# Low-rank and gate weights of an RWKV-7 mixer split in two once, kept in DRAM, and multiplied in one-pass products

## Chip, core and metric

The kernel runs on one core of one Trainium2 chip. The metric is the device time of one execution in microseconds (us). TensorE (PE in the profile) does the matrix products, VectorE (DVE), ScalarE (ACT) and GpSimd (POOL) the elementwise work; SyncE (SP) and ACT issue transfers (DMA).

## What is computed

One layer of a hybrid decoder for 256 prompt tokens and 8 tokens of sequences that go on, 264 columns in all: a SwiGLU feed-forward (2048 to 5504 to 2048), a mixing stage in which sliding-window attention and an RWKV-7 recurrence stand side by side, and a second feed-forward. The part that the change is about, cut from the reference:

```python
wl, al, gl = xm[..., o3:o4], xm[..., o4:o5], xm[..., o5:]          # 64, 64 and 128 columns
w = -softplus(-(w0 + tanh(wl) @ w2)) - 0.5                         # w2: 64 x 1024, decay
logw = -exp(w)
a = sigmoid(a0 + al @ a2)                                          # a2: 64 x 1024, rate
g = sigmoid(gl) @ g2                                               # g2: 128 x 1024, gate
...
out = (yn + bonus) * g
```

All numbers are float32, so each weight matrix is used at nearly float32 precision.

## The kernel before

Activations lie transposed: 128 features in the partitions, 264 tokens along a row. A weight block of 128 x 128 is the stationary side of a product, the 264 tokens the moving side.

**Large products** (`gemm`, with `chunk`) split both sides. `chunk` loads up to 512 columns of weights (256 KB) on SP's queue into a ring `raw` of 6, rounds them on ACT into `hi` (type fp32r, which TensorE takes in one pass), and subtracts `hi` on DVE to get `lo`; `hi` and `lo` are rings of 4 tiles each. The activations are split in the same way, once, by the norms. Each 128 x 128 block then takes three one-pass products (line 84 in the profile, as all products): hi by hi, hi by the activations' low part, lo by hi. A full chunk feeds 12 products. As the rings have 4 tiles, a chunk's rounding can start as soon as PE has finished with the fourth chunk before it.

**The first feed-forward** runs in six parts (`PARTS`) of 7 or 8 blocks of the inner width. For each block f it multiplies 2 x 16 weight blocks (gate and up), then for the part the down projection. From the second part on, each f also copies one row block of the key and value caches from DRAM to DRAM on ACT's queue (`copy_one`, line 230), 16 copies in all.

**The mixing stage** (`mixing_body`) projects the normed input tile by tile (`win`, `shifted`), in the order of the list `SEQ`. The first two tiles are the low-rank and gate inputs: `la` (64 rows for decay, 64 for rate) and `sgl`. `tw` gets tanh of the first 64 rows of `la`, and a 65th row of ones that adds w0; `sgl` gets the sigmoid. The 16 heads are worked in 8 pairs, two pairs to a batch. For each pair a task `prep` loads its weights with `load` (a ring `ld` of `NLD` = 6 tiles, from SP's queue) and makes two plain float32 products, `zp` (decay, 65 rows) and `ap` (rate, 128 rows of which 64 are zero in the weights). Each batch's `chain` then solves a triangular system with many small DVE steps (tiles X, Xt, st, TT, PT), and its `gnorm` at the end makes one float32 gate product `gp` per pair. All small products write to a ring `m` of 5 PSUM banks, the large ones to a ring `acc` of 3.

**Order.** Tasks are generators; `tick` after each chunk of a large product advances each by one step, and constants such as `PW`, `PZ` and `LAG` say how many ticks a task waits. From this text a scheduler of the tile framework, with its own timing of engines, orders each engine's instructions. `high_priority` puts a weight chunk's steps ahead of others. Each engine then runs its list in order, waiting on semaphores.

The lines of the float32 products and of the loads:

```python
lw = load(I["lw"][p], (P, 256))
mm(zp[:, :T], lw[0:65, 0:P], tw[0:65, :])
mm(ap[:, :T], lw[:, P:2 * P], la)
...
mm(gp[:, :T], g2s[k], sgl)
```

Of the kernel before, what the change touches and what calls it, by code (L numbers as in the profile page):

```python
# [28 lines left out]
NACC, NM = 3, 5  # L29
NH, NQ, NT, NLD = 16, 8, 16, 6  # L30
ROW = 320
# [19 lines left out]
VG1, VGM, VG2, VGF = 0, 16, 32, 48  # L51
VMU, VKK, VKA, VA0, VRK, VLW, VLB, VSK, VSD = 64, 90, 98, 106, 114, 122, 130, 138, 154
NVEC = 155
CID, CBO, CCM, CMK = 0, 128, 256, 384


def body(tc, I, O):
# [51 lines left out]
    with ExitStack() as ctx:  # L109
# [21 lines left out]
        def mp():  # L131
            return pp.tile([P, 512], F32, tag="m", bufs=NM, name=uid("m"))
# [95 lines left out]
        def copy_one():  # L228
            n, c, b = copies.pop()
            tc.keep_in_program_order(A.dma_start(O[n][b, 0:127, :], I[c][b, 1:128, :]))  # L230

        def hblock(nf):
            h = cur[0][0].tile([P, max(PARTS), 2, ROW], F32R, tag="h", bufs=2, name=uid("h"))
            return [(h[:, k, 1, :T], h[:, k, 0, :T]) for k in reversed(range(nf))]

        def ffn(nrm, xr, gu, dn, nxt, load, begin=None, side=None, ready=None, end=None):
            rstd = None
            f0 = 0
            for pi, nf in enumerate(PARTS):
# [25 lines left out]
                for f in range(f0 + n0 if first else f0, f0 + nf):  # L265
# [9 lines left out]
                    if begin and pi and copies:  # L275
                        copy_one()
                    if side and pi:
                        next(side, None)
# [90 lines left out]
        def mixing_body(mx, n2, n3, XD, XR):  # L369
            def fix(shape, name):  # L370
                return mx.tile(list(shape), F32, name=name)
# [15 lines left out]
            wc = fix((P, NPAIR, 4), "wc")  # L387
            tw = fix((65, T), "tw")
            G.memset(tw[64:65, :], 1.0)
            rs = fix((P, T), "rs")  # L390
# [5 lines left out]
            for i in range(4):  # L396
                G.tensor_copy(unit[i * 32:i * 32 + 32, :], ident[i * 32:i * 32 + 32, i * 32:i * 32 + 32])
            half = fix((P, 16), "half")
            ts(V, half, vec[:, VKA:VKA + 16], 0.5, ALU.mult)
            less = fix((P, 8), "less")  # L400
# [28 lines left out]

            la, sgl = fix((P, T), "la"), fix((P, T), "sgl")  # L430

# [6 lines left out]
            def prep(p, bt, k, xrr, xk, xv):  # L438
                lw = load(I["lw"][p], (P, 256))
                zp = mp()  # L440
                mm(zp[:, :T], lw[0:65, 0:P], tw[0:65, :])
                ap = mp()
                mm(ap[:, :T], lw[:, P:2 * P], la)
                sg, a = tmp(), tmp()
                act(sg, zp[:, :T], AF.Tanh, scale=0.5)
                ts(G, sg, sg, 0.5, ALU.mult, 0.5, ALU.add)
# [116 lines left out]
            def chain(bt):  # L563
# [119 lines left out]
                for k in range(n):  # L683
                    A.dma_start(O["wkvp"][bt.p0 + k], S[:, k])
                g2s = [load(I["g2"][bt.p0 + k], (P, P)) for k in range(n)]
                yield from gnorm(bt, pY, N, g2s)
# [15 lines left out]
            def gnorm(bt, pY, N, g2s):  # L702
# [26 lines left out]
                for k in range(n):  # L729
                    p, o = bt.p0 + k, yb[bt.p0 + k]  # L730
                    gp = mp()
                    mm(gp[:, :T], g2s[k], sgl)
                    o4, b4 = (x[:, :NP].rearrange("p (q e t) -> p q e t", q=2, e=2) for x in (o, bt.bv[k]))
                    t4 = tp[:, k * NP:(k + 1) * NP].rearrange("p (q g t) -> p q g t", q=2, g=2)
                    for e in range(2):
                        for h in range(2):
                            r = HALF[h]
                            stt(o4[r, :, e, :], t4[HALF[e], :, 1 - h, :], vc(VLW + p)[r], b4[r, :, e, :], ALU.mult, ALU.add)
                    stt(o[:, NP:], sq[:, k * NB:(k + 1) * NB], vc(VLW + p), bt.bv[k][:, NP:], ALU.mult, ALU.add)
                    stt(o, o, vc(VLB + p), gp[:, :T], ALU.add, ALU.mult)  # L740
                    mixed[p] = o
# [162 lines left out]

            shifted(0, la)
            act(tw[0:64, :], la[0:64, :], AF.Tanh)
            shifted(1, sgl)
            act(sgl, sgl, AF.Tanh, scale=0.5)
            ts(G, sgl, sgl, 0.5, ALU.mult, 0.5, ALU.add)
            bat, att, bts, scores = [], [], [], []  # L910
            for kind, i in SEQ:
# [84 lines left out]
        def second_ffn(n3, xr, XR):  # L996
# [6 lines left out]
            with tc.tile_pool(name="f2", bufs=1) as fp:  # L1003
# [70 lines left out]
                for e, q, o, n, r in ((V, SP, 0, 1, rp[:, :T]), (V, A, 1, 3, rp[:, :T]), (G, SP, 4, 4, rb), (V, A, 12, 4, rp[:, :T])):  # L1074
# [3 lines left out]
                    q.dma_start(O["yT"][:, d:d + n, :], y)  # L1078

        xsp = [dp.tile([P, T], F32, tag=f"xsp{o}", name=f"xsp{o}") for o in range(KD)]  # L1080
        xs4 = [blk(f"x{i}", 8, F32R) for i in (3, 2, 1, 0)]
# [36 lines left out]
def layout(i):  # L1118
# [3 lines left out]
    for n in (1, 2):  # L1122
# [12 lines left out]
        v(i["ffn1_norm"][0]), v(i["mix_norm"][0]), v(i["ffn2_norm"][0]), v(i["final_norm"]),  # L1135
        v(i["shift_mu"][0][sc]), v(i["key_k"][0]), v(i["key_a"][0]), v(i["aaa_a0"][0]),
        v(i["bonus_r_k"][0].reshape(-1)), v(i["ln_x_w"][0]), v(i["ln_x_b"][0]),
# [6 lines left out]
    a["shs"] = c(i["state_shift"][0][:, sc].reshape(NB, NSH, P).transpose(2, 1, 0))  # L1144
    lw = np.zeros((8, P, 256), f4)
    lw[:, :64, :P] = i["decay_w2"][0].reshape(64, 8, P).transpose(1, 0, 2)
    lw[:, 64, :P] = i["decay_w0"][0].reshape(8, P)
    lw[:, 64:, P:] = i["aaa_a2"][0].reshape(64, 8, P).transpose(1, 0, 2)
    a["lw"] = lw
    a["g2"] = c(i["gate_g2"][0].reshape(P, 8, P).transpose(1, 0, 2))  # L1150
    bk = _buckets()
# [39 lines left out]
```

## Time and profile before

| | |
|---|---|
| median of 3 runs | 1935.38 us (1935.24 to 1937.05) |
| profiled execution, its own time | 1934.77 us |
| its span, first to last instruction | 1932.9 us |
| granted TensorE clock | 0.998 of full |
| first feed-forward | to about 757 us |
| mixing stage with its output projection | about 757 to 1236 us |
| second feed-forward and final norm | from about 1236 us |
| moved by DMA | 357 MB, 185 GB/s |

A row of a timeline reads: start in us, duration in us, engine, line of the kernel, operation, output tile <- input tiles (buffer numbers left out), shapes, and how many instructions were merged. In brackets stands how long the engine sat idle before, and what released it. Matmul rows overlap, since a product is shown until its last column has left the array: what one costs is read from start to start. A float32 product is recorded as two rows. "PEld" is the loading of the stationary side. "SPq" and "ACTq" rows are the issue of a transfer, not the transfer.

### The profile page before, as it was taken

Reading aid. Unit: us, or ns where it says so; the run is one execution under the profiler, and the core shown is the slowest. Engines: PE = TensorE matmul, PEld = TensorE weight load, DVE = VectorE, ACT = ScalarE, POOL = GpSimd, SP = SyncE. Lnnn points to the kernel's source line nnn. Section 1 sums busy time; section 2 is a strip of 40 time slices with the busy share of each in tenths; the row PEclk is TensorE's granted clock in tenths of the full one; section 3 lists DMA queues with packets and bytes.
Section 4 is the critical chain, followed back from the end, with each engine's and each line's share of the span. In section 5 each row is a group of like instructions: output and inputs, shape, how many; then the busy total and the mean of one; then the engine's idle time right before and its main releaser. Section 6 shows DMA issues by size and latency. Waiting matters only on the chain.

```text
span 1932.9 us, 45519 instructions
## 1 busy us (share of the span) xinstructions
PE 1919.4 (99%) x17171; PEld 1897.1 (98%) x17171; DVE 1311.8 (68%) x2606; ACT 1023.7 (53%) x2034; POOL 260.1 (13%) x376
## 2 busy tenths in 40 slices
PE   9999999999999999999999999999999999999998
PEld 9999999999999999999989999999999999999998
DVE  5865555655556568889988977866666666666665
ACT  5644444444444457675657555644444444444446
POOL 0401101011010113222102100300101001010012
PEclk9999999999999999999999999999999999999999
DMA  7666666666666668555646656666666666666664
GB/s 241 178 192 196 185 195 195 183 192 177 190 183 180 188 181 238 177 165 153 176 120 165 210 155 183 175 188 188 189 195 195 186 192 189 194 195 184 193 181 150
DMA packets 218464, 357.27 MB, mean 185 GB/s; under 512 B 33516, under 2 KB 71804, under 8 KB 218244
## 3 DMA queue, kind: packets, MB, share of 16 engines
q1 hardware_dynamic: 211936, 346.02, 60.8%
q10 hardware_dynamic: 6308, 8.35, 1.4%
q8 instruction: 134, 2.20, 0.4%
q14 instruction: 86, 0.70, 0.1%
HBM read 346.67 MB, written 9.69 MB: 184 GB/s over the span
## 4 chain that ended last, share of the span: by engine, by line
PE 96%; DVE 1%; ACT 1%; issue 1%; DMA 0%; POOLq 0%; POOL 0%; ACTq 0%; DVEq 0%
PE acc L84 89%; PE m L84 6%; DVE lo L68 0%; ACT t L78 0%; ACT hi L141 0%; DMA x<-in_x 0%; DVE t L801 0%; DVE st L68 0%; DVE Xt L68 0%; DMA ld<-in_bias 0%; ACT BT L533 0%; ACT L78 0%; POOLq L1187 0%; DVE PT L68 0%; PE m L528 0%
## 5 line engine op out<-in xcount | busy, mean ns | idle before, releaser
L68 DVE TENSOR_TENSOR lo<-raw,hi 128x512 fp32r<-128x512 f32 (+1 forms) x1288 | 874.0, 682 | 510.4 <-ACT hi L141 486.9
L141 ACT CAST hi<-raw 128x512 fp32r<-128x512 f32 (+1 forms) x1288 | 776.8, 606 | 820.2 <-PE acc L84 745.2
L84 PE MATMUL acc<-x,hi 128*128 128x264 f32 x4840 | 893.4, 286 | 0.8 <-ACT hi L141 0.8
L84 PEld LDWEIGHTS acc<-x,hi 128*128 128x128 f32 x4840 | 750.1, 189 | 4.3 <-ACT hi L141 1.0
L84 PE MATMUL acc<-x,lo 128*128 128x264 f32 x2420 | 691.3, 286 | 0.2 <-DVE lo L68 0.2
L84 PE MATMUL acc<-h,hi 128*128 128x264 f32 x2752 | 495.0, 284 | 0.0
L84 PEld LDWEIGHTS acc<-x,lo 128*128 128x128 f32 x2420 | 457.2, 189 | 2.7 <-issue 0.7
L84 PEld LDWEIGHTS acc<-h,hi 128*128 128x128 f32 x2752 | 424.4, 189 | 0.0
L84 PE MATMUL acc<-h,lo 128*128 128x264 f32 x1376 | 387.8, 284 | 0.0
L84 PEld LDWEIGHTS acc<-h,lo 128*128 128x128 f32 x1376 | 259.2, 189 | 0.0
L68 POOL TENSOR_TENSOR t<-t,t 128x264 f32<-128x264 f32 x74 | 79.8, 1078 | 1096.1 <-DVE t L68 949.8
L84 PE MATMUL acc<-y,hi 128*128 128x264 f32 x648 | 122.7, 284 | 0.0
L84 PE MATMUL acc<-o,hi 128*128 128x264 f32 x648 | 120.1, 284 | 0.0
L84 PE MATMUL acc<-kv,hi 128*128 128x264 f32 x582 | 109.8, 285 | 0.0
L84 PEld LDWEIGHTS acc<-y,hi 128*128 128x128 f32 x648 | 101.2, 189 | 0.1
L84 PEld LDWEIGHTS acc<-o,hi 128*128 128x128 f32 x648 | 100.1, 189 | 0.0
L71 DVE SCALAR_TENSOR_TENSOR x<-acc,x 128x264 f32<-128x264 f32 (+1 forms) x193 | 81.1, 425 | 24.3 <-PE acc L84 23.4
L84 PE MATMUL acc<-y,lo 128*128 128x264 f32 x324 | 92.0, 284 | 0.0
L84 PE MATMUL acc<-o,lo 128*128 128x264 f32 x324 | 92.0, 284 | 0.0
L84 PEld LDWEIGHTS acc<-kv,hi 128*128 128x128 f32 x582 | 89.9, 189 | 0.2
L68 DVE TENSOR_TENSOR t<-acc,t 128x264 f32<-128x264 f32 x156 | 67.4, 432 | 32.9 <-PE acc L84 32.9
L84 PE MATMUL acc<-kv,lo 128*128 128x264 f32 x291 | 82.9, 285 | 0.0
(307 smaller groups left out, 1592.5 us busy)
## 6 DMA issues: line engine op xcount, KB each, us to landing
raw<-in_gu SPq DMA_DIRECT2D x688, 256.0 KB, 3.4
raw<-in_dn SPq DMA_DIRECT2D x224, 256.0 KB, 2.9
raw<-in_win SPq DMA_DIRECT2D x152, 256.0 KB, 3.4
raw<-in_dn SPq DMA_DIRECT2D x160, 192.0 KB, 2.8
raw<-in_wout SPq DMA_DIRECT2D x64, 256.0 KB, 3.5
xsp<-x ACTq DMA_DIRECT2D x16, 132.0 KB, 3.4
x<-xsp SPq DMA_DIRECT2D x16, 132.0 KB, 4.2
ld<-in_sT SPq DMA_DIRECT2D x16, 128.0 KB, 3.6
```

Of the source, the lines that this page charges most:

```text
L68: return e.tensor_tensor(out=out, in0=a, in1=b, op=op)
L71: return V.scalar_tensor_tensor(out=out, in0=a, scalar=s, in1=b, op0=op0, op1=op1)
L84: return TE.matmul(out, lhsT, rhs, start=start, stop=stop, **k)
L141: A.copy(hi[:, :w], raw[:, :w])
```

## The change

Three things. The weights of the three small products are put in one tensor `low` of 128 x 3072: eight pairs of 256 columns, the decay and rate weights of each pair, each of the two stacked twice over the 128 rows (64 rows and the same 64 again), then 1024 columns of the gate. While the first feed-forward is in its fourth part, six calls of `low_one` take it through `chunk` in pieces of 512 columns and store both parts in a DRAM tile `low`. In mixing, the inputs are split too: `lor[0]` holds the high part of tanh(wl) in rows 0 to 63 and its low part in rows 64 to 127, `lor[1]` the same for `al`; `gate[0]` and `gate[1]` are the high and low part of the gate's input. A pair's decay and rate products are then two one-pass products each (the high and the low weights by the stacked input), the gate's are three. w0 comes in as a bias of the tanh on ACT, halved in advance. `NLD` is 8 instead of 6, and each load fetches one part (128 KB).

```diff
-NH, NQ, NT, NLD = 16, 8, 16, 6
+NH, NQ, NT, NLD = 16, 8, 16, 8
...
+        lows = list(range(6))
+
+        def low_one():
+            q = lows.pop(0)
+            for e, x in enumerate(chunk(I["low"][:, q * 512:(q + 1) * 512], CH, V)):
+                A.dma_start(low[:, 2 * q:2 * q + 2, e], x.bitcast(F32).rearrange("p (k c) -> p k c", k=2))
...
                     if begin and pi and copies:
                         copy_one()
+                    if begin and pi > 2 and lows:
+                        low_one()
...
-            tw = fix((65, T), "tw")
-            G.memset(tw[64:65, :], 1.0)
...
-            half = fix((P, 16), "half")
-            ts(V, half, vec[:, VKA:VKA + 16], 0.5, ALU.mult)
+            half = vec[:, VKA:VKA + 24]
+            ts(V, half, half, 0.5, ALU.mult)
...
-            la, sgl = fix((P, T), "la"), fix((P, T), "sgl")
+            lor = blk("e", 2, F32R)
+            gate = [mx.tile([P, T], F32R, name=f"gate{i}") for i in range(2)]
+
+            def parts(src):
+                return [load(src[:, e], (P, 256)).bitcast(F32R) for e in range(2)]
...
-                lw = load(I["lw"][p], (P, 256))
-                zp = mp()
-                mm(zp[:, :T], lw[0:65, 0:P], tw[0:65, :])
-                ap = mp()
-                mm(ap[:, :T], lw[:, P:2 * P], la)
+                lw = parts(low[:, p])
+                zp, ap = mp(), mp()
+                for j, ps in enumerate((zp, ap)):
+                    for i, w in enumerate(lw):
+                        mm(ps[:, :T], w[:, j * P:(j + 1) * P], lor[j], i == 0, i == 1)
                 sg, a = tmp(), tmp()
-                act(sg, zp[:, :T], AF.Tanh, scale=0.5)
+                act(sg, zp[:, :T], AF.Tanh, scale=0.5, bias=half[:, 16 + p:17 + p])
...
-                g2s = [load(I["g2"][bt.p0 + k], (P, P)) for k in range(n)]
+                g2s = parts(low[:, NPAIR + bt.i])
...
-                    mm(gp[:, :T], g2s[k], sgl)
+                    c = slice(k * P, (k + 1) * P)
+                    mm(gp[:, :T], g2s[0][:, c], gate[0], True, False)
+                    mm(gp[:, :T], g2s[0][:, c], gate[1], False, False)
+                    mm(gp[:, :T], g2s[1][:, c], gate[0], False, True)
...
-            shifted(0, la)
-            act(tw[0:64, :], la[0:64, :], AF.Tanh)
-            shifted(1, sgl)
+            la = shifted(0, tmp())
+            act(la[0:64, :], la[0:64, :], AF.Tanh)
+            for r, x in zip(HALF, lor):
+                A.copy(x[0:64], la[r])
+                tt(V, x[64:128], la[r], x[0:64].bitcast(F32), ALU.subtract)
+            sgl = shifted(1, tmp())
             act(sgl, sgl, AF.Tanh, scale=0.5)
             ts(G, sgl, sgl, 0.5, ALU.mult, 0.5, ALU.add)
+            A.copy(gate[0], sgl)
+            tt(V, gate[1], sgl, gate[0].bitcast(F32), ALU.subtract)
...
+        low = dp.tile([P, NPAIR + len(BATCH), 2, 256], F32, tag="low", name="low")
```

The scheduler makes a new order of it. Three places follow; `hi_`, `raw_` and the like with a number are single buffers of the rings. First ACT's list where the fourth part of the first feed-forward begins, before and then now:

```order
L141 CAST hi_5337<-raw_5336 128x512
L141 CAST hi_5355<-raw_5354 128x384
L230 DMA out_ks<-in_ck 16x2032
L141 CAST hi_5375<-raw_5374 128x512
L141 CAST hi_5393<-raw_5392 128x512
```

```order
L141 CAST hi_5338<-raw_5337 128x512
L141 CAST hi_5356<-raw_5355 128x384
L230 DMA out_ks<-in_ck 16x2032
L141 CAST hi_5376<-raw_5375 128x512
L237 DMA low<-hi_5376 128x2x256
L141 CAST hi_5384<-raw_5383 128x512
L237 DMA low<-lo_5377 128x2x256
L141 CAST hi_5402<-raw_5401 128x512
```

The first chunk after the cache copy is now one of the split weights; its high part is stored at once, its low part behind the next chunk's cast. The five further splits stand in the same way, one in each of the following five blocks f.

Second, ACT's list at the start of the mixing stage, before and then now. The tile `la` is `t_10482` in the changed kernel, `e` is the tile of `lor`:

```order
L78 ACTIVATE la<-pj_10406,vec 128x256
L141 CAST hi_10638<-raw_10637 128x512
L78 ACT_TABLE_LOAD
L78 ACTIVATE tw<-la 64x264
L141 CAST hi_10656<-raw_10655 128x512
L78 ACTIVATE sgl<-pj_10407,vec 128x256
L141 CAST hi_10681<-raw_10680 128x512
L78 ACTIVATE sgl<-sgl 128x264
L141 CAST hi_10699<-raw_10698 128x512
```

```order
L78 ACTIVATE t_10482<-pj_10453,vec 128x256
L433 COPY t_10570<-ss 128x8
L141 CAST hi_10693<-raw_10692 128x512
L78 ACT_TABLE_LOAD
L78 ACTIVATE t_10482<-t_10482 64x264
L922 CAST e_10475<-t_10482 64x264 x2
L141 CAST hi_10711<-raw_10710 128x512
L78 ACTIVATE t_10570<-pj_10454,vec 128x256
L433 COPY t_10654<-ss 128x8
L141 CAST hi_10736<-raw_10735 128x512
L78 ACTIVATE t_10570<-t_10570 128x264
L141 CAST hi_10754<-raw_10753 128x512
```

Two casts of 64 x 264 now stand between the tanh and the weight cast behind it. On DVE the two subtractions of 64 x 264 stand ahead of that chunk's subtraction.

Third, PE's list in the first batch, from the last of its Gram products (`kr` by `bk`) to the transposes of `kr` and `bk` (lines 521 and 528 before, 532 and 539 now); rows of `acc` are large products. Before and then now:

```order
L84 MATMUL m_11379<-kr_11262,bk_11261 128x128
L84 MATMUL acc_11345<-x_108,hi_11427 128x264
L84 MATMUL acc_11345<-x_108,lo_11428 128x264
L84 MATMUL acc_11345<-x_108,hi_11427 128x264 x2
L84 MATMUL acc_11345<-x_108,lo_11428 128x264
L84 MATMUL acc_11345<-x_108,hi_11427 128x264 x2
L84 MATMUL acc_11345<-x_108,lo_11428 128x264
L84 MATMUL acc_11345<-x_108,hi_11427 128x264 x2
L84 MATMUL acc_11345<-x_108,lo_11428 128x264
L521 MATMUL m_11444<-C,kr_10968 128x128 x2
L528 MATMUL m_11451<-C,bk_10967 128x128 x4
```

```order
L84 MATMUL m_11442<-kr_11325,bk_11324 128x128
L532 MATMUL m_11507<-C,kr_11027 128x128 x2
L84 MATMUL acc_11408<-x_110,lo_11541 128x264
L84 MATMUL acc_11408<-x_110,hi_11540 128x264 x2
L84 MATMUL acc_11408<-x_110,lo_11541 128x264
L84 MATMUL acc_11408<-x_110,hi_11540 128x264 x2
L84 MATMUL acc_11408<-x_110,lo_11541 128x264
L539 MATMUL m_11514<-C,bk_11026 128x128 x4
```

The Gram products stand 13 large products later than before, and the first transposes follow them at once instead of after 11 large products. The small products of the other batches move by up to about 16 large products.

More of the change, by code (lines that the diff above doesn't have):

```diff
@@ L51 @@
 VG1, VGM, VG2, VGF = 0, 16, 32, 48
-VMU, VKK, VKA, VA0, VRK, VLW, VLB, VSK, VSD = 64, 90, 98, 106, 114, 122, 130, 138, 154
-NVEC = 155
+VMU, VKK, VKA, VA0, VW0, VRK, VLW, VLB, VSK, VSD = 64, 90, 98, 106, 114, 122, 130, 138, 146, 162
+NVEC = 163
 CID, CBO, CCM, CMK = 0, 128, 256, 384
@@ L1135, in layout @@
         v(i["ffn1_norm"][0]), v(i["mix_norm"][0]), v(i["ffn2_norm"][0]), v(i["final_norm"]),
-        v(i["shift_mu"][0][sc]), v(i["key_k"][0]), v(i["key_a"][0]), v(i["aaa_a0"][0]),
+        v(i["shift_mu"][0][sc]), v(i["key_k"][0]), v(i["key_a"][0]), v(i["aaa_a0"][0]), v(i["decay_w0"][0].reshape(-1)),
         v(i["bonus_r_k"][0].reshape(-1)), v(i["ln_x_w"][0]), v(i["ln_x_b"][0]),
@@ L1144, in layout @@
     a["shs"] = c(i["state_shift"][0][:, sc].reshape(NB, NSH, P).transpose(2, 1, 0))
[L1145 to L1150, printed above, removed]
+    w2, a2 = (i[n][0].reshape(64, 8, P) for n in ("decay_w2", "aaa_a2"))
+    low = np.stack([np.concatenate([x, x], 0) for x in (w2, a2)], 2).reshape(P, 2 * 8 * P)
+    a["low"] = c(np.concatenate([low, i["gate_g2"][0]], 1))
     bk = _buckets()
```

## Prediction

> **What bounds the kernel now.** I read the page's busy times first, then its chain of work, then a table of busy times by stage, then the waits of TensorE (PE).
>
> ```profile
> PE 1919.4 (99%) x17171; PEld 1897.1 (98%) x17171; DVE 1311.8 (68%) x2606; ACT 1023.7 (53%) x2034; POOL 260.1 (13%) x376
> PE 96%; DVE 1%; ACT 1%; issue 1%; DMA 0%; POOLq 0%; POOL 0%; ACTq 0%; DVEq 0%
> 66.00:757.00 691.00, 691.00 (x5760) 691.00 (x5759) 418.99 (x711) 344.28 (x619) 89.45 (x89) 1.00 0.64 190
> 757.00:870.00 113.00, 112.85 (x1042) 110.16 (x1042) 92.20 (x191) 76.93 (x186) 30.62 (x79) 1.00 0.61 179
> 870.00:990.00 120.00, 117.72 (x1558) 110.19 (x1555) 110.80 (x371) 75.27 (x203) 20.51 (x52) 1.00 0.55 156
> 990.00:1100.00 110.00, 109.40 (x1240) 100.77 (x1239) 94.15 (x278) 73.72 (x202) 19.07 (x45) 1.00 0.61 173
> 1100.00:1180.00 80.00, 80.00 (x879) 78.39 (x878) 62.86 (x136) 38.74 (x70) 1.02 (x1) 1.00 0.59 165
> PE m L808 <- DVE PT L68: 1.2, 1, 1.2
> PE m L755 <- issue: 0.7, 1, 0.7
> PE m L84 <- ACT kr L544: 0.2, 1, 0.2
> ```
>
> In the table by stage the columns are stretch, length, then busy us (and instructions) of PE, PEld, DVE, ACT and POOL, then PEclk, DMA share and GB/s. PE is the bound: 99% of the span is busy and 96% of the chain is its own work, at the full clock. The first feed-forward (up to 757) has no idle PE at all. The mixing stage (757 to 1180), where the low-rank and gate products are, has about 3 us of it, in single waits such as the three shown. So a shorter product on PE shortens the program, as long as no other engine is late for what comes next. DVE is the nearest: 110.8 of 120 us busy between 870 and 990.
>
> **Removed and added products.** Eight channel pairs have two FP32 products each (decay and rate) and one for the gate: 24 in all. These rows show four of them in a row, two of the gate and the two of pair 6 (a product leaves two records).
>
> ```profile
> 1028.35 1.06 PE L84 MATMUL m<-sgl,ld 128*128 128x264 f32 x4
> 1029.24 0.61 PE L84 MATMUL m<-tw,ld 65*128 65x264 f32 x2
> 1029.69 0.61 PE L84 MATMUL m<-la,ld 128*128 128x264 f32 x2
> 1029.94 0.48 PE L84 MATMUL acc<-x,lo 128*128 128x264 f32 x1
> 1030.25 0.40 PE L84 MATMUL acc<-x,hi 128*128 128x264 f32 x2
> ```
>
> From start to start, two gate products take 1029.24 - 1028.35 = 0.89 us, the decay product 1029.69 - 1029.24 = 0.45: 0.445 each. A one-pass product takes 691.00 / 5760 = 0.120 us, its weight load hidden beside the one before; this is also the form of every added product (128 rows, 264 columns). Removed: 24 x 0.445 = 10.7 us. Added: decay and rate 2 each per pair, since high and low halves of the activations lie stacked over 128 rows, and 3 for the gate: 8 x (2 + 2 + 3) = 56, times 0.120 = 6.7 us. On PE that is **-4.0 us**: -0.41 per pair for decay and rate, -0.085 for the gate.
>
> The rows say that FP32 costs 3.7 times one pass. [...]
>
> **The weights' split in the first feed-forward.** Six more chunks go through the rings raw, hi and lo: 6 loads on SP's queue, 6 casts on ACT, 6 subtractions on DVE, 12 stores on ACT's queue. PE multiplies nothing with them. Each takes one of four hi/lo slots, so PE's weights are ready one chunk later than now.
>
> ```profile
> 389.74 0.62 ACT L141 CAST hi<-raw 128x512 fp32r<-128x512 f32 x1 [0.82 <-PE acc L84]
> 390.39 0.69 DVE L68 TENSOR_TENSOR lo<-raw,hi 128x512 fp32r<-128x512 f32 x1 [0.75 <-ACT hi L141]
> 391.18 0.62 ACT L141 CAST hi<-raw 128x512 fp32r<-128x512 f32 x1 [0.82 <-PE acc L84]
> 401.82 0.52 ACTq L230 DMA_DIRECT2D out_ks<-in_ck  x1
> out_ks<-in_ck ACTq DMA_DIRECT2D x8, 127.0 KB, 3.9
> X<-sa SPq DMA_DIRECT2D x4, 512.0 KB, 4.8
> 320.00:343.00 23.00, 23.00 (x194) 23.00 (x194) 12.77 (x21) 11.36 (x21) 4.29 (x4) 1.00 0.64 194
> ```
>
> A cast starts when PE gives a slot back, every 391.18 - 389.74 = 1.44 us. Three other chunks are then ahead of it: 3 x 1.44 = 4.32 us, of which cast and subtraction take 390.39 + 0.69 - 389.74 = 1.34. So 2.98 us are to spare, and 1.54 with one slot lent out (about 1.0 for the first of the six, which follows the narrower chunks of the down projection). The slot comes back when its stores have landed. The low part's store stands behind the next cast in ACT's queue, so it issues by 1.44 + 0.62 + 0.52 = 2.6 us after the split's cast; landing in 3.9 to 4.8 (the rows of the 127 KB copies and of a 512 KB transfer; these have 256 KB), that is 6.5 to 7.4. The chunk that reuses the slot needs it by 6 x 1.44 + 0.24 - 0.69 = 8.2, so landings up to about 5.6 us cost nothing. Behind the store that waits for DVE stand ACT's later casts, which have the same 1.5 us. I take **0**. The cover is this look-ahead; if it were gone, each chunk would cost its 1.34 us, 8.0 in all, the upper end. The copies of the caches, which share this stage (320 to 343), left PE 23.00 of 23.00 busy.
>
> **The start of mixing.** Here ACT and DVE get new work while PE's weights are scarce.
>
> ```profile
> 763.16 0.51 ACT L78 ACTIVATE la<-pj,vec 128x256 f32<-128x256 f32 x1 [1.79 <-DVE pj L68]
> 763.58 0.60 ACT L141 CAST hi<-raw 128x512 fp32r<-128x512 f32 x1
> 764.20 1.28 ACT L78 ACT_TABLE_LOAD   x1
> 765.49 0.43 ACT L78 ACTIVATE tw<-la 64x264 f32<-64x264 f32 x1
> 765.82 0.60 ACT L141 CAST hi<-raw 128x512 fp32r<-128x512 f32 x1
> 766.46 0.69 DVE L68 TENSOR_TENSOR lo<-raw,hi 128x512 fp32r<-128x512 f32 x1 [1.21 <-ACT hi L141]
> 767.41 0.40 PE L84 MATMUL acc<-x,hi 128*128 128x264 f32 x2
> 767.65 0.28 PE L84 MATMUL acc<-x,lo 128*128 128x264 f32 x1
> ```
>
> The cast at 765.82 ends 0.99 us before PE's first product with it (767.41), and its subtraction ends at 767.15, only 0.50 before the first low product (767.65). In the changed order two casts of 64x264 stand between the tanh and this cast, and two subtractions of 64x264 before its subtraction; also one copy of 8 columns, which stood at 757 before, comes ahead. No row has such a cast; the nearest is the tanh of the same size, 0.33 to the next start and 0.43 in all. That puts the weight cast 0.7 to 1.0 us later. Its high products still come in time or nearly; the subtraction then ends at 767.9 to 768.2 instead of 767.15, and PE waits 0.2 to 0.6 us. The bounds are 0 (if the table load comes earlier) and 1.2 (if the next chunk is late too). I take **+0.4**. Later gate cast and subtraction meet casts with over 1 us to spare: nothing.
>
> **Waits that take part of the gain.** At pairs 2 and 4 PE waits between the decay and the rate product:
>
> ```profile
> 825.79 0.51 ACT L78 ACTIVATE t<-pj,vec 128x256 f32<-128x256 f32 x1
> 826.21 0.60 ACT L141 CAST hi<-raw 128x512 fp32r<-128x512 f32 x1
> 826.34 0.71 PE L84 MATMUL m<-tw,ld 65*128 65x264 f32 x2
> 826.77 0.38 ACT L544 COPY kr<-m 128x256 f32<-128x256 f32 x1
> 827.20 0.71 PE L84 MATMUL m<-la,ld 128*128 128x264 f32 x2
> ```
>
> 0.86 us pass from one to the other instead of 0.45, since the PSUM bank is given back by the ACT copy that ends at 827.15. ACT comes to it without a gap from its copies before (825.79, 826.21), so a shorter decay product waits longer: of its 0.21 us nothing comes, twice, and DVE's dense stretch after 870 may take as much. Against that, PE's transposes and the copies behind them now stand closer together, which lets ACT start a little earlier. Between 0 and +0.8 I take **+0.2**. The loads of two parts instead of one (16 for 8, and 8 for 8 of the gate) go through 8 slots instead of 6, each pair waiting for the same release as one load did: nothing, with up to 0.5 us if SP falls behind.
>
> **Sum.** -4.0 + 0.4 + 0.2 = -3.4. From the profiled execution (1934.77 us: span 1932.9 and 1.9 around it) that gives 1931.4; the median of the three runs shown is 0.6 higher, 1935.38, so **1932.0**. The time outside the span and the end of the program stay.
>
> **Rivals.** (1) *The whole gain arrives*: the start's casts fit, and an earlier ACT frees the banks. For it: no wait of PE in the stage is longer than 1.2 us now, and these may shrink, since the scheduler also moves the small products by some ten gemm products (the third place under the change shows such a move). Against: 0.50 us to spare at 767. Time 1931.2, to 1929.8 with shorter waits. (2) *Other engines eat the gain* in 757 to 1180: DVE's chains of small steps set the pace (92% busy in 870 to 990), and PE only waits longer. Against: in that stage PE still idles just 2.3 of 120 us. 1933.5 to 1935.4. (3) *Slower*: the split's stores hold the slots too long. Each of the six splits moves 768 KB in a column of 11.52 us, 67 GB/s beside the 194 that flow there; if a store lands in 8 us, PE waits 8.0 - 5.6 = 2.4 us at each, +14.4 in all, so 1946.4. It decides the sign from 5.6 + 3.4/6 = 6.2 us. Against: four times the size of a cache copy took only 4.8 us.
>
> [...]
>
> (4) *The products do not run in one pass* though the weights are rounded in advance: 56 x 0.445 - 10.7 = +14.2, 1949.6. The rounded weights come back from DRAM as plain 32-bit words and are only renamed; but the hi and lo weights of all gemms have the same form and show 0.120.
>
> **Chances.** Forecast 0.45, whole gain 0.30, eaten 0.18, slower by the stores 0.05, not one pass 0.02. A measurement of this kernel tells about 0.2%, 3.9 us, from no change, so the bound is 1931.5: the whole gain lies beyond it, and so does about a fifth of the forecast's spread (0.10). Faster 0.40, within 0.53, slower 0.07. The range, 1929.8 to 1935.6, takes in the forecast, the whole gain and most of the eaten case.
>
> **What would show it.** Right: products from e and gate 0.12 us apart; PE without waits up to 757 and the second feed-forward beginning 3 to 4 us earlier; at 767 a wait for DVE's lo of some tenths. Wrong: PE waiting for hi or lo around the six splits; records of e or gate 0.22 us apart; PE's idle time in mixing grown by over 1 us, on DVE or a PSUM bank.

## The result: slower by 0.7%

| | before | after |
|---|---|---|
| median | 1935.64 us (1935.12 to 1937.05, 6 runs) | 1948.86 us (1947.45 to 1950.71, 6 runs) |
| profiled execution, its own time | 1934.77 us | 1947.45 us |
| its span | 1932.9 us | 1945.7 us |
| start of the 6,101st weight product, in the first feed-forward's last down projection | 740.05 us | 750.17 us (+10.1) |
| from there to the 8,701st, near the end of the mixing stage's projections | 426.94 us | 429.48 us (+2.5) |

The ratio is 1.0067, with a 95% interval of 1.0054 to 1.0080. The two last lines compare the start of the same two weight products (of 264 columns, counted from the start) in both traces; below, "the mixing stage" is the stretch between these two. The second feed-forward is unchanged. So the loss stands at two places: 10.1 us in the first feed-forward, where nothing had been expected, and 2.5 us in the mixing stage, where 3.4 us of gain had been.

From the page after: busy times, and the first line of the chain of work.

```profile
PE 1921.9 (99%) x17179; PEld 1898.0 (98%) x17179; DVE 1316.4 (68%) x2615; ACT 1026.7 (53%) x2043; POOL 251.0 (13%) x375
PE 93%; DMA 3%; ACT 2%; DVE 2%; issue 1%; POOLq 0%; ACTq 0%; POOL 0%; SPq 0%; DVEq 0%
```

PE's own share of the chain fell from 96% to 93%, and DMA has 3% where it had 0. The loss does not show in the busy times: PE, DVE and ACT are within 5 us of before, POOL has 9 us less. The table by stage does (stretch, length, busy us and instructions of PE, PEld, DVE, ACT, POOL, then PEclk, DMA share, GB/s):

```profile
387.00:470.00 83.00, 76.31 (x610) 73.78 (x609) 45.07 (x71) 37.34 (x69) 10.31 (x11) 1.00 0.72 223
470.00:757.00 287.00, 287.00 (x2394) 287.00 (x2393) 175.44 (x305) 145.03 (x267) 35.99 (x37) 1.00 0.64 188
870.00:990.00 120.00, 115.99 (x1554) 109.09 (x1553) 108.44 (x360) 71.38 (x189) 19.09 (x51) 0.99 0.55 156
990.00:1110.00 120.00, 118.18 (x1335) 108.53 (x1334) 102.28 (x310) 82.52 (x230) 17.91 (x48) 0.99 0.60 171
```

PE idles 6.7 us in 387 to 470, the stretch of the six splits, and not at all in 470 to 757. In the mixing stage the granted clock is 0.99, where every stage had 1.00. The waits of PE (engine, tile and line, released by, us in total, times, longest):

```profile
PE acc L84 <- ACT hi L141: 6.2, 6, 2.2
PE m L84 <- ACT BT L544: 2.2, 2, 1.6
PE m L84 <- ACT W L621: 1.6, 1, 1.6
PE acc L84 <- DVE lo L68: 1.5, 7, 0.2
PE m L822 <- DVE PT L68: 1.3, 1, 1.3
```

Only the last of these had a counterpart of its size before.

**The first feed-forward.** The chain of waits in order of time (start, us, what):

```profile
397.14 6.65 DMA low<-hi
403.79 0.02 issue
403.81 0.62 ACT hi L141
404.44 0.03 issue
404.46 0.70 DVE lo L68
405.16 0.04 issue
405.21 5.71 PE acc L84 x45
```

The two groups of stores among the transfers (engine, count, KB, median us to landing):

```profile
low<-hi ACTq DMA_DIRECT2D x6, 256.0 KB, 5.2
low<-lo ACTq DMA_DIRECT2D x6, 256.0 KB, 5.6
```

A store of a high part is issued at 397.14 and lands 6.65 us later; only then ACT makes its next cast, at 403.81, then DVE the subtraction, and PE goes on at 405.21. So a store's landing is on the path that sets the end. PE's rows at this place:

```profile
404.48 0.52 PE L84 MATMUL acc<-x,hi 128*128 128x264 f32 x2 [2.19 <-ACT hi L141]
405.21 0.39 PE L84 MATMUL acc<-x,lo 128*128 128x264 f32 x1 [0.21 <-DVE lo L68]
```

Behind the idle 2.19 us the next four products start 0.2 to 0.5 us apart instead of 0.120, the first low one waiting for `lo`; their rows overlap and count as busy. Counted by the starts of the same products, the six splits cost 0.9, 3.0, 1.7, 1.7, 1.5 and 1.3 us, which are the 10.1.

At five of the six splits the cast that waits is not the fourth behind the split's own but the second (at the first split it is the third), as ACT's list of instructions shows, here at the second split (buffer numbers kept, semaphores in brackets):

```
386 L237 DMA low_90<-hi1037_5540 128x2x256 [waits Activation_49]
387 L141 CAST hi1040_5548<-raw1039_5547 128x512 [waits DMAHW4_49,PE_49]
388 L237 DMA low_90<-lo1038_5541 128x2x256 [waits DVE_49]
389 L141 CAST hi1043_5566<-raw1042_5565 128x512 [waits DMAHW5_49,DMAHW1_49]
390 L141 CAST hi1046_5584<-raw1045_5583 128x512 [waits DMAHW6_49,PE_49]
```

The casts at 387 and 390 wait for their loads and for PE, which frees a buffer. The one at 389 waits for two transfers and not for PE: its load, and the store issued at 386. The scheduler gave the buffer of the split chunk to the second chunk after it. By the prediction's own figures this moves the point of decision: the store is issued 0.64 us after the split's cast begins, and the second cast behind it has to run by 2 x 1.44 + 1.54 = 4.4 us, so landings up to about 3.8 us cost nothing, not 5.6. The landings that are waited for took 4.87 to 6.65 us, late at every split. At the last five, landing less loss is 3.5 to 3.7 us, close to the 3.8 of this estimate.

**The mixing stage.** ACT's timeline around one of the longest new waits of PE (start, us, engine, line, operation, tiles, shapes, count, idle time before and its releaser):

```profile
956.84 1.14 ACT L141 CAST hi<-raw 128x512 fp32r<-128x512 f32 x2 [5.51 <-PE acc L84]
957.88 0.36 ACT L774 COPY kv<-m 128x256 f32<-128x256 f32 x1
958.14 0.25 ACT L777 COPY t<-m 8x128 f32<-8x128 f32 x1
958.42 0.36 ACT L621 COPY W<-m 32x256 f32<-32x256 f32 x1
958.80 0.36 ACT L621 COPY W<-m 32x256 f32<-32x256 f32 x1
```

PE's timeline at the same place:

```profile
956.93 0.28 PE L84 MATMUL acc<-x,hi 128*128 128x264 f32 x1
958.83 1.14 PE L84 MATMUL m<-TT,W 32*32 32x32 f32 x32 [1.62 <-ACT W L621]
```

Two weight casts wait until 956.84 for PE to release a buffer, and the W copies that PE needs next stand behind them in ACT's list. Before:

```profile
943.15 1.14 ACT L141 CAST hi<-raw 128x512 fp32r<-128x512 f32 x2 [2.01 <-DVE t L68]
944.73 0.75 ACT L610 COPY W<-m 32x256 f32<-32x256 f32 x2
```

There a pair of casts stood ahead of the same copies too, but ran 3.6 us earlier (203.1 us after the 6,101st weight product, now 206.7), did not wait for PE, and PE did not wait. It is not the same pair: in ACT's rows 644 weight casts stand ahead of these W copies before, and 651 now, which is one more than the six of the splits. And behind this wait, and behind the one of 1.64 us for BT (1068.34 to 1069.98), the granted clock fell from 1.00 to 0.50 (table by stage, in stretches of 3.41 us):

```profile
956.29:959.70 3.41, 1.65 (x39) 1.32 (x38) 2.21 (x7) 2.79 (x7) 0.00 (x0) 1.00 0.27 80
959.70:963.12 3.42, 3.42 (x27) 2.96 (x21) 3.21 (x17) 3.39 (x12) 0.00 (x0) 0.50 0.87 244
1068.93:1072.34 3.41, 2.36 (x13) 1.73 (x14) 1.48 (x7) 2.95 (x10) 0.84 (x4) 1.00 0.72 188
1072.34:1075.76 3.42, 3.42 (x18) 3.42 (x17) 2.77 (x12) 2.13 (x8) 1.00 (x3) 0.50 0.87 242
```

For 3.41 us each, PE was granted half its clock, right after a stretch of 3.41 us in which it was busy 1.65 and 2.36 us; products of 264 columns start 0.22 us apart there (1072.37, 1072.59) instead of 0.120. Compared product by product with the same kinds at full clock, these two cost an estimated 1.1 to 2.1 and 1.7 us; the first is uncertain because most of its products are small ones.

### The profile page after: what moved, and what is told of

Same layout as the page of the kernel before. It is cut to its first block, busy times and chain, and to the rows that moved or that the text cites. A ratio compares the mean times of both kernels' runs of the same rounds, so it can differ in the third digit from the quotient of the medians.

```text
span 1945.7 us, 45617 instructions
## 1 busy us (share of the span) xinstructions
PE 1921.9 (99%) x17179; PEld 1898.0 (98%) x17179; DVE 1316.4 (68%) x2615; ACT 1026.7 (53%) x2043; POOL 251.0 (13%) x375
## 4 chain that ended last, share of the span: by engine, by line
PE 93%; DMA 3%; ACT 2%; DVE 2%; issue 1%; POOLq 0%; ACTq 0%; POOL 0%; SPq 0%; DVEq 0%
PE acc L84 86%; PE m L84 6%; DMA low<-hi 2%; ACT hi L141 1%; DVE lo L68 1%; DMA Xt<-sa 0%; ACT kr L535 0%; ACT t L78 0%; DMA x<-in_x 0%; ACT BT L544 0%; DVE y L71 0%; DVE gm L68 0%; DMA ld<-in_kc 0%; DVE Xt L68 0%; DMA raw<-in_win 0%
```

## Experiments: the first feed-forward

Theory A: the store holds a buffer, and the second cast behind the split waits for its landing. Rival B: the six chunks take time on DMA, ACT or DVE. Ratios are to the kernel before on the same chip.

**e1, buffers of their own.** The split chunk no longer uses the rings hi and lo:

```
-            for e, x in enumerate(chunk(I["low"][:, q * 512:(q + 1) * 512], CH, V)):
+            with tc.high_priority():
+                raw = wp.tile([P, CH * P], F32, tag="raw", bufs=NRAW, name=uid("raw"))
+                hi, lo = (cur[0][0].tile([P, CH * P], F32R, tag="sp", bufs=4, name=uid("sp")) for _ in range(2))
+                SP.dma_start(raw, I["low"][:, q * 512:(q + 1) * 512])
+                A.copy(hi, raw)
+                tt(V, lo, raw, hi.bitcast(F32), ALU.subtract)
+            for e, x in enumerate((hi, lo)):
```

> The changed kernel, but the two parts of a split chunk are written to four buffers of their own instead of buffers of the hi and lo rings; the casts, subtractions and the 12 stores of 256 KB stay. Theory A (a buffer of the hi ring is held by its store, and the second chunk after it waits for that store to land): the 6 long PE waits of the first feed-forward go, about 9 to 10 us, and the time is 1938 to 1940 us; landing of a store stays 5 to 6.6 us. Rival B (the stores' traffic, or ScalarE's and VectorE's six more casts and subtractions, delay the weight loads or casts): the first feed-forward keeps its 10 us, the time stays 1947 to 1950 us.

1939.58 us (before 1934.99), ratio 1.0020 (1.0011 to 1.0029). The first feed-forward in its table by stage:

```profile
387.00:470.00 83.00, 83.00 (x694) 83.00 (x693) 48.17 (x80) 42.41 (x76) 12.51 (x12) 1.00 0.75 242
```

Its stores among the transfers:

```profile
low<-sp ACTq DMA_DIRECT2D x12, 256.0 KB, 5.2
```

PE is busy 83.00 of 83.00, with the same stores landing as late as in the changed kernel, and with more DMA traffic in the stretch (0.75 against 0.72). The 6,101st weight product starts at 740.00, where the kernel before has 740.05. Traffic and engine work cost nothing; the held buffer cost all 10.1 us of the first feed-forward. What is left, 4.6 us, is the mixing stage's, which is 5.0 us longer than before in this profile and was 2.5 in the changed kernel's: with the same small products, PE waits 2.8 us for PT there instead of 1.3 (below, e8).

**e4, the splits alone**, added to the kernel before, without any use of what they store:

```
+        lows = list(range(6))
...
+        def low_one():
+            q = lows.pop(0)
+            for e, x in enumerate(chunk(I["low"][:, q * 512:(q + 1) * 512], CH, V)):
+                A.dma_start(low[:, 2 * q:2 * q + 2, e], x.bitcast(F32).rearrange("p (k c) -> p k c", k=2))
...
+                    if begin and pi > 2 and lows:
+                        low_one()
```

> The kernel before, with the changed kernel's splits and stores in the first feed-forward added and nothing else: the mixing stage computes as before and does not read what is stored. Theory A: the first feed-forward is 9 to 11 us longer and the mixing stage is unchanged, 1945 to 1947 us. A rival that puts the loss into the mixing stage: within 1 us of before, 1935 to 1936.5 us.

1945.00 us, ratio 1.0050 (1.0037 to 1.0064), as theory A has it. In its profile the 6,101st weight product starts 12.1 us late, with waits of 3.1 and 1.8 us there. The granted clock from 387 to 470 us is 0.96, where the changed kernel's is 1.00; that is as much as two stretches of 3.41 us at half clock (2 x 3.41 x 0.50 / 83 = 0.04), and one of them follows the wait of 3.1 us (last section). The mixing stage itself is within 0.3 us of before.

**e5, longer runs in DRAM.**

```
-                A.dma_start(low[:, 2 * q:2 * q + 2, e], x.bitcast(F32).rearrange("p (k c) -> p k c", k=2))
+                A.dma_start(low[:, q, e], x.bitcast(F32))
```

> The changed kernel with the parts laid out in DRAM so that each partition stores one run of 2 KB instead of two of 1 KB; same bytes, same order of instructions, same buffers. Theory A: the loss goes with the landing time of the store. If the landing falls from 5.2 to 4.5 us, each of the six waits falls by as much and the time to about 1944 us; if the landing does not change, neither does the time (1947 to 1950 us). Rival B (ScalarE and VectorE work): no change in the first feed-forward whatever the landing.

1948.03 us, ratio 1.0072 (1.0058 to 1.0086). The landing did not fall (median 5.4 us for the high part, 6.0 for the low), and neither did the time. It tells nothing between A and B; runs of 2 KB instead of 1 KB did not shorten these stores. In its profile (1946.17 us) the first feed-forward loses 8.4 us, on landings of 4.87 to 6.27 us.

**e9, five buffers instead of four.**

```
-CH, NRAW, NHL = 4, 6, 4
+CH, NRAW, NHL = 4, 6, 5
-NH, NQ, NT, NLD = 16, 8, 16, 8
+NH, NQ, NT, NLD = 16, 8, 14, 6
```

> The changed kernel with five buffers instead of four in each of the hi and lo rings (and 14 temporary and 6 load buffers in the mixing stage instead of 16 and 8, to make room). In ScalarE's list it is still the second chunk after a split one that gets the store's buffer. Theory A (that chunk waits for the store to land): casts run one chunk, 12 products or 1.44 us, further ahead, so each of the six waits in the first feed-forward is up to 1.44 us shorter, and its loss falls from 10 to about 2 to 4 us. Rival B (contention, engine work): no change there, 10 us. The mixing stage: theory C gives no number, since its order changes.

1945.56 us, ratio 1.0057 (1.0040 to 1.0073). In its profile the first feed-forward loses 5.7 us instead of 10.1. Rival B had no change; theory A's size was missed by 2 to 4 us, and the landings were later here (5.7 and 6.2 us in the median, 0.5 more). Two of its six splits cost nothing, the other four 0.6 to 2.0 us.

## Experiments: the mixing stage

Theory C: with shorter products the scheduler puts weight casts, copies and products in another order, and that order waits. Rivals D and E put the loss on one of the two edits, H on what the change adds (loads, casts, dependences), G on the number of buffers. All but e11 have e1's own buffers, so that their first feed-forward costs nothing.

**e6 and e7, one edit at a time**, the other group of products as in the kernel before. In e6:

```
-                g2s = parts(low[:, NPAIR + bt.i])
+                g2s = [load(I["g2"][bt.p0 + k], (P, P)) for k in range(n)]
...
-                    mm(gp[:, :T], g2s[0][:, c], gate[0], True, False)
-                    mm(gp[:, :T], g2s[0][:, c], gate[1], False, False)
-                    mm(gp[:, :T], g2s[1][:, c], gate[0], False, True)
+                    mm(gp[:, :T], g2s[k], sgl)
```

In e7:

```
-                lw = parts(low[:, p])
+                lw = load(I["lw"][p], (P, 256))
...
-                        mm(ps[:, :T], w[:, j * P:(j + 1) * P], lor[j], i == 0, i == 1)
+                mm(zp[:, :T], lw[0:65, 0:P], tw[0:65, :])
...
+                mm(ap[:, :T], lw[:, P:2 * P], la)
```

> The changed kernel with four buffers of their own for the split chunks (as in e1), and of the products only those of decay and rate in one pass; the gate's as in the kernel before (FP32, weights from the input). Theory C (the mixing stage loses because the shorter products move weight casts and other copies ahead of the copies that TensorE waits for; which of them depends on the schedule as a whole): its products' gain is at most 4.7 to 2.2 us of decay and rate, and the waits at about 947 and 1059 us may be there or not; 1935 to 1940 us. Rival D (it is the decay's and rate's edit alone, through the load or the two stacked parts): 1939 to 1941 us as in e1, with e7 near 1934. Rival E (it is the gate's edit alone): 1933 to 1935 us here, e7 near 1939.

> As e6 the other way round: own buffers for the split chunks, the gate's products in one pass from the stored parts, those of decay and rate as in the kernel before (FP32), and six load buffers as there. Theory C: 1934 to 1940 us, with or without the waits. Rival D: 1934 to 1935.5 us. Rival E: 1938 to 1940 us.

Decay and rate alone: 1937.16 us, ratio 1.0005 (0.9996 to 1.0014); gate alone: 1940.29 us, 1.0020 (1.0011 to 1.0029). Of the rivals E comes nearest, but its reason fails: in e6's profile the mixing stage is still 3.2 us longer than before, with a wait for W of 2.0 us and one for PT of 2.4 us, though no gate product changed. The gate's edit has next to no gain to lose, either: the 24 products take 3.46 us from start to start, the 8 FP32 ones 2.88, or about 3.7 with what they add to the product behind them (last section).

**e8, W first.** Two casts are tied behind the W copies of the second batch:

```
+                if latecast and latecast[0] in (6, 7):
+                    tc.add_manual_dep(i.ins, latecast[1].ins.name, mybir.DependencyInfo(mybir.DependencyClass.NoSync, mybir.DependencyReason.SCHED_ONLY))
```

> e1 with one difference: in the second batch two weight casts, which wait for buffers that TensorE frees later, stand behind the two W copies in ScalarE's list instead of ahead of them. Theory C: the wait of 1.6 us before the products TT times W at 947 us goes, and with it the stretch of half clock behind it (about 1.7 us), if that is caused by the wait; 1.6 to 4 us faster than e1, 1935.5 to 1938 us. Rival F (the wait only moves to the two casts' own products, or the clock drops in any case): within 0.7 us of e1.

1940.85 us, ratio 1.0025 (1.0015 to 1.0035): rival F. The longest waits of PE in the stage, first e1's, then e8's:

```profile
PE m L828 <- DVE PT L68: 2.8, 1, 2.8
PE m L84 <- ACT BT L550: 2.2, 2, 1.6
PE m L84 <- ACT W L627: 1.6, 1, 1.6
```

```profile
PE m L834 <- DVE PT L68: 3.0, 1, 3.0
PE m L84 <- ACT BT L554: 2.3, 2, 1.8
PE m L84 <- ACT W L631: 0.5, 1, 0.5
```

The wait for W fell from 1.6 to 0.5 us, so most of it was due to the casts ahead of the copies. The longer wait for PT stayed, 3.0 us against 2.8, and the one for BT rose from 1.6 to 1.8. PE's idle time in the stage fell from 7.8 to 7.2 us, and the stages with the waits for PT (870 to 990) and BT (990 to 1110) have a granted clock of 0.99 and 0.97 in e1, of 0.99 and 0.99 in e8. In the profile the stage is 0.7 us shorter than e1's; in the time no gain shows.

**e10, e11 and e12, a fifth buffer**: for e1, for the kernel before (with 13 temporary buffers), and for e6. In the kernel before:

```
-CH, NRAW, NHL = 4, 6, 4
+CH, NRAW, NHL = 4, 6, 5
-NH, NQ, NT, NLD = 16, 8, 16, 6
+NH, NQ, NT, NLD = 16, 8, 13, 6
```

> e1 (own buffers for the split chunks) with five buffers in the hi and lo rings (14 temporary and 6 load buffers). If the mixing stage loses because weight casts wait for one of only four buffers and hold up the copies behind them (theory G), the waits at about 947, 964 and 1059 us shrink, and the time falls to 1933 to 1936 us. If it loses because the order of ScalarE's and VectorE's lists fits the products' old durations only (theory C), there are other waits of the same size, and the time stays at 1937 to 1941 us.

> The kernel before with five buffers in the hi and lo rings (13 temporary buffers): what the fifth buffer is worth without the change. Theory G: 1 to 2 us faster than before at most, since its mixing stage waits only 3.0 us. Theory C: its mixing stage, too, is rescheduled, and may gain or lose 3 us.

> e6 (own buffers, decay and rate in one pass, the gate as before) with five buffers in the hi and lo rings. If a version of the change can beat the kernel before, it is the one without the gate's edit, whose products did not get shorter (3.46 us against 2.88 us), and without waits for buffers: 1933 to 1935 us by theory G; 1935 to 1940 us by theory C.

e10: 1938.50 us, 1.0014 (1.0005 to 1.0023). e11: 1943.46 us, 1.0042 (1.0027 to 1.0057). e12: 1940.98 us, 1.0032 (1.0021 to 1.0043). Theory G's times are not reached: none of the three comes near the time it expects, and e11 and e12 are slower than without the fifth buffer. To make room each also has fewer temporary buffers (13 or 14 for 16), and e10 and e12 have 6 load buffers for 8, so what the fifth buffer does by itself is not shown. The kernel before, unchanged but for this and 3 temporary buffers less, loses 7.8 us in its mixing stage, more than theory C had allowed for: 3.2 of them are more idle time, and the mean granted clock over the span is 0.996, where the kernel before has 0.998. Its longest waits of PE there are new ones:

```profile
PE m L84 <- ACT kr L524: 1.5, 1, 1.5
PE acc L84 <- ACT kv L978: 1.0, 1, 1.0
PE m L84 <- DMA ld<-in_cv: 1.0, 1, 1.0
```

So another order can cost this stage several us also where no product changed.

**e13, the old length.** e1, with useless repeats of products, so that PE has as much work for each pair as before and the scheduler orders ACT's list around the second batch as it did:

```
-                    for i, w in enumerate(lw):
-                        mm(ps[:, :T], w[:, j * P:(j + 1) * P], lor[j], i == 0, i == 1)
+                    for i, w in enumerate(lw + lw):
+                        mm(ps[:, :T], w[:, j * P:(j + 1) * P], lor[j], i % 2 == 0, i % 2 == 1)
...
+                    mm(gp[:, :T], g2s[0][:, c], gate[0])
```

> e1 (own buffers for the split chunks, all products in one pass), but each product of decay and rate is made twice and one of the gate's three is made twice, the first time for nothing, so that TensorE has as much to do per pair as in the kernel before; ScalarE's list then stands around the second batch as it does there. 40 one-pass products more than e1 at 0.12 us are 4.8 us more work on TensorE. Theory C (the mixing stage loses because shorter products change the order in which weight casts, copies and products stand, and that order waits): the waits at 947 us (1.63 us) and 964 us (2.80 us, 1.19 in the kernel before) go back to what they are in the kernel before, and most of the half clock with them: although it does 4.8 us more, it is no slower than e1, 1936 to 1940 us, and TensorE's idle time in the mixing stage falls from 7.8 us to 3 to 5 us. Rival H (the waits come from what the change adds: more loads, casts, dependences on two parts): the waits stay and the time is 1943 to 1945 us.

1938.56 us, ratio 1.0013 (1.0004 to 1.0022), against e1's 1.0020 with 40 products fewer. The same place in ACT's timeline:

```profile
944.02 1.14 ACT L141 CAST hi<-raw 128x512 fp32r<-128x512 f32 x2 [2.31 <-DMA Xt<-sa]
945.60 0.75 ACT L627 COPY W<-m 32x256 f32<-32x256 f32 x2
```

Its waits of PE, and then its table by stage:

```profile
PE m L84 <- ACT kr L561: 1.6, 2, 1.4
PE m L829 <- DVE PT L68: 1.2, 1, 1.2
```

```profile
870.00:990.00 120.00, 117.79 (x1591) 110.87 (x1588) 110.17 (x369) 76.20 (x203) 19.58 (x52) 1.00 0.54 162
```

The casts run at 944.02 instead of 946.5 (e1), the W copies end 1.3 us before PE comes to them (947.65), the wait for PT is the 1.2 us of before, and the clock is 1.00. PE's idle time in the stage is 4.3 us, against 7.8 in e1 and 3.0 before. Two parts, more loads and more casts are all still there, so rival H falls.

The order can be counted in the rows. Ahead of the second batch's W copies ACT has 644 weight casts before and in e13, and 645 in e1; ahead of the first product of TT and W there PE has 7,213 large products before and in e13, and 7,228 in e1. Of the runs with four buffers, every one with that one more cast (the changed kernel, e1, e5, e6, e14) waits 0.6 to 2.0 us for W, and those with 644 (before, e4, e7, e13; the splits' own casts not counted) do not. That the order makes this wait is shown by this and by e8. No run has the short products in the old order, so how much of the other waits comes from PE being earlier, by the time that its short products save, is not separated.

**e14, longer pauses.** e6 with two constants of the chain's spacing (PZ and P2 of the second batch) from 4 to 5:

```
-P2 = (2, 4, 1, 1)
+P2 = (2, 5, 1, 1)
-PZ = (2, 4, 2, 4)
+PZ = (2, 5, 2, 4)
```

> e6 (own buffers, decay and rate in one pass, the gate as before) with one chunk of weight products more between two steps of the second batch's chain at two places (PZ and P2 of batch 1 from 4 to 5), where TensorE waited 2.0 and 2.4 us in e6. Theory C: the steps' distances, counted in chunks, are too short for the shorter products; the two waits shrink to below 1 us each and the time falls by 1 to 3 us, to 1934 to 1936 us. Rival H or a chain that only ends later: within 1 us of e6's 1937.

1940.20 us, ratio 1.0023 (1.0014 to 1.0032): no faster than e6, against theory C's number. The wait for PT fell from 2.4 to 1.1 us, but the wait for W only from 2.0 to 1.6, and the one for BT, a hundred us later, grew from 0.8 to 1.7. Moving these two steps moved others behind them. No version of the change tried here beats the kernel before; the nearest, e6, cannot be told from it.

## Why the prediction was wrong

The forecast was 1932.0 us, the range ended at 1935.6; the time was 1948.9, slower. For its first step, the changed kernel's rows of one pair's four decay and rate products:

```profile
792.15 0.64 PE L84 MATMUL m<-e,ld 128*128 128x264 f32 x4
792.63 0.40 PE L84 MATMUL acc<-x,hi 128*128 128x264 f32 x2
```

By its own steps:

- **Products, -4.0 us: right.** These four take 792.63 - 792.15 = 0.48 us, 0.12 each, so rival 4 (not one pass) is out. The sum can be worked out with e13, whose stage has a granted clock of 1.00 throughout: it is 1.95 us longer than before, 1.22 of that is more idle time, so its products cost 0.73 more than before; the changed kernel has 40 products fewer, 40 x 0.120 = 4.8 us, which makes -4.1.
- **The weights' split, 0: wrong by 10.1 us, the step that decided the sign.** It said that "the chunk that reuses the slot needs it by 6 x 1.44 + 0.24 - 0.69 = 8.2, so landings up to about 5.6 us cost nothing". That took for granted that buffers go round in turn. ACT's list, which stands before any run, gave the buffer to the second chunk at five of the six splits, not the fourth; the limit was about 3.8 us. The estimate of the landing, 3.9 to 4.8 us, was low as well (5.2 and 5.6 in the median), but even its lower end was just beyond that limit. e1 shows the held buffer alone to be the cause, and e4 that the splits alone bring the loss.
- **Rival 3, slower by the stores, 0.05:** the right mechanism, at the wrong threshold: it saw no loss up to 5.6 us, a change of sign from 6.2 and 14.4 us of loss at 8; the loss of 10.1 came from landings of 4.87 to 6.65. The time, 1948.9, near its 1946.4, is in part luck: that sum has the stores at 8 us and the mixing stage's gain, and neither came.
- **The start of mixing, +0.4:** the step there is +0.2, measured at the same weight products between 772 and 782 us. **Bank waits, +0.2:** the two between the decay and the rate product are gone; ahead of the decay product of pair 2 PE now waits 0.56 us.
- **The mixing stage as a whole: wrong.** "Other engines eat the gain" (rival 2) named the stage and the engines, but its worst case was the loss of the gain. The gain of 4.1 us is outweighed by 3.4 us more idle time (6.4 against 3.0) and an estimated 2.8 to 3.8 us of half clock: +2.1 to +3.1, where +2.5 was measured. That the shorter products give the scheduler another order was seen (the moves under the change), and counted only as a chance of shorter waits. For the wait for W the order is shown to be the cause, by e8 and by the counts under e13; for the stage as a whole e13 points to it. Which step of the order is the first to go wrong isn't settled: e8 and e14, which moved single steps, shortened single waits and gained no time.
- **Rival 1's time:** the sum without its two additions, 1932.0 - 0.6, is 1931.4, not 1931.2. The rows at 1029 us are those of pair 7, not 6, which changes no sum.

## What to carry to other kernels

A buffer that is stored from belongs in a pool of its own: in the rings that feed PE here, the stores' landing of 4.87 to 6.65 us joined the path and cost 10.1 us, and with buffers of their own (e1) it cost nothing. Which chunk waits for such a landing is to be read from the built order, not from the ring's length. Where a scheduler orders several engines by its own durations, a shorter instruction is a new schedule: look for the in-order copies and casts ahead of what the bound engine needs, and try the old durations with the new instructions, as in e13, to tell the order from the new parts. Two waits of PE amid small products, of 1.62 and 1.64 us, were each followed here by 3.41 us of half clock, an estimated 1.1 to 2.1 us more: such a wait is to be read together with the clock behind it.

## What the hardware showed unexpectedly

**The granted clock fell to 0.50 for 3.41 us at a time.** In the changed kernel's mixing stage it did so from 959.70 and from 1072.34 us, at the estimated 1.1 to 2.1 and 1.7 us given above. Between 757 and 1110 us the tables by stage of before, e4 and e13 have 1.00 throughout; those of the changed kernel, e1, e5, e6, e7 and e8 have 0.97 to 0.99 in one or two stages. PE had idled for a part of the 3.41 us ahead of each of the two, but half clock did not follow every such idle time: in the changed kernel, a wait of 2.19 us in the first feed-forward (402.29 to 404.48) lies across two stretches of 3.41 us, and both were followed by the full clock, as its table by stage shows:

```profile
399.92:403.33 3.41, 2.37 (x20) 2.15 (x18) 0.00 (x0) 0.00 (x0) 0.00 (x0) 1.00 0.66 227
403.33:406.75 3.42, 2.06 (x14) 1.84 (x15) 2.29 (x5) 2.18 (x4) 0.51 (x1) 1.00 0.20 40
```

In e4 a wait of 3.10 us lies in one such stretch, and the next had half the clock:

```profile
414.86:418.27 3.41, 0.52 (x2) 0.30 (x2) 0.67 (x2) 1.32 (x3) 0.00 (x0) 1.00 0.44 161
418.27:421.69 3.42, 3.34 (x15) 3.34 (x16) 2.90 (x6) 1.87 (x4) 1.78 (x2) 0.50 0.58 154
```

The wait of 1.62 us for W (up to 958.83) was followed by half clock 0.87 us after its end, at 959.70. Busy time alone does not tell these cases apart: 2.36 of 3.41 us was followed by the half clock at 1072.34, 2.06 of 3.42 from 403.33 wasn't. In e6 even 2.87 us, in 101 products, was:

```profile
824.20:827.61 3.41, 2.87 (x101) 2.57 (x101) 1.38 (x4) 3.29 (x12) 0.48 (x3) 1.00 0.59 180
827.61:831.03 3.42, 3.42 (x18) 3.42 (x17) 1.62 (x4) 3.02 (x8) 2.14 (x8) 0.50 0.74 200
```

What decides it, these rows do not settle.

**The FP32 products cost more than their own records here.** From start to start, the 24 FP32 products' records sum to 9.8 us and the 56 one-pass ones to 8.2, a difference of 1.6. The rest stands at the product behind: at 12 places a one-pass product follows the last FP32 record, and there it takes 0.32 us to the next start instead of 0.12 (the prediction's rows have one from 1029.94 to 1030.25), 12 x 0.20 = 2.4 us. Together that is 4.0, close to the 4.1 found in the whole stage. Behind the one-pass products of the changed kernel the same step takes 0.12 to 0.13.

**The landing of these transfers did not follow their size alone.** 256 KB from SBUF to DRAM took 5.2 (high parts) and 5.6 us (low parts) in the median beside the weight stream, 4.87 to 6.65 where PE's path waited for it; in the kernel before, cache copies of 127 KB took 3.9 and loads of 512 KB 4.8 us.
